# Two transformer blocks in one kernel: the order of the two kinds of weight products on TensorE

## The chip, the cores and the metric

One NeuronCore of a Trainium2 chip runs the whole program. Times are device microseconds (us) of that core. The kernel before took 2190.84 us, the median of 3 runs (2190.77 to 2191.94).

## What is computed

The input is one sequence of 256 positions with 2048 features. It passes through two residual blocks and a last RMS norm.

The first block normalises x and projects it to 3584 features. Those feed a gated causal convolution of width 3, a trailing mean minus the token followed by a small grouped product, and an attention of 4 heads over a memory of 256 positions. The memory's keys and values are a product of their own. The joined 2048 features go through `w_out` and are added to x. A feed-forward part follows: a product with 2 x 5632 columns, a causal convolution of width 3 with a bias, `silu(gate) * value`, and a product back to 2048 columns.

The second block has 8 heads of an attention over three dilated windows and 8 heads of a "difference" attention (two softmaxes, one subtracted from the other, then a norm), `w_out_2`, and a feed-forward part without the convolution.

```
x = x + mix(rmsnorm(x)) @ w_out
x = x + (silu(gate) * val) @ w_down        # gate, val = split(conv(rmsnorm(x) @ w_up))
x = x + concat(dilated(x), diff(x)) @ w_out_2
x = x + (silu(h @ w_gate) * (h @ w_up)) @ w_down
return rmsnorm(x)
```

All inputs are float32. Nearly all of the work is the weight products with 256 moving positions.

## The kernel before, in words

**Two halves for one float32 product.** Each weight block of 128 x 128 is split on the chip into an upper part (`hi`, rounded to the matmul format by a copy on ScalarE, line 175) and a lower part (`lo`, raw weight minus upper part, a subtraction on VectorE, line 187). Activations are kept as pairs too: 256 columns of upper part and 256 columns of lower part side by side, 512 columns in all. A block then needs two matmuls into one PSUM accumulator of 512 columns. The *long* one (line 208) multiplies `hi` with all 512 columns. The *short* one (line 211) multiplies `lo` with the 256 upper columns, and adds to the accumulator's second half. An accumulator's first matmul is a long one that starts it, and its last is a long one that closes it. I call a long and a short matmul on one weight block, together, a block.

**Units and quarters.** Weights come in units of 16 blocks, 1 MB each, by one DMA into `raw` (3 buffers, line 164). Half a unit, 8 blocks, is what one `hi` tile (4 buffers) and one `lo` tile (4 buffers) hold. The program is written out by hand in quarters: in each quarter, `emit_all` (lines 1009 to 1034) first lets evictions and other follow-up work that is due go out (`stage`), then the splitting of weights that are needed one or two units later, then 4 blocks of matmuls through `products`, then extra matmuls that are due (attention scores, transposes, norm sums). The queue of an engine holds its instructions in that order, and each engine works its own queue off in order.

**The order inside `products`.** It is called with the 4 blocks of a quarter. A flag, `longs`, says whether the last call ended in long matmuls or in short ones, and the next call begins with the same kind; so 4 + 4 long matmuls and 4 + 4 short ones follow one another, in runs of 8, save in quarters where an accumulator is opened or closed. There a run may be of 1, 4 or 7.

**What follows a sum.** When the quarter with the closing matmul is over, a generator (`done`, posted by `ws_units`, line 255, for the next quarter) evicts the accumulator: ScalarE copies one half, VectorE adds the other (lines 416 to 418), and further steps go out in later quarters. For residual sums VectorE alone does it (lines 742 and 743). `ready` keeps evictions back until a norm's factor is there. The accumulators are 4 PSUM buffers. The order of the products of a stage (`late_order`) takes the last two inputs of the first two sums late, so that the stage before can finish them.

**Attention of the second block.** Heads are started at fixed quarters (`t0`, lines 959 and 965), beside the next stages' products. The value products use another form (`vs_unit`, lines 275 to 277) that isn't touched.

Of the kernel before, what the change touches and what calls it, by code (L numbers as in the profile page):

```python
# [10 lines left out]
F32 = mybir.dt.float32  # L11
# [7 lines left out]
P = 128  # L19
D = 2048  # L20
S = 256
KT = D // P
# [4 lines left out]
UB = 16  # L27
EPS = 1e-6
SUBLN_EPS = 1e-5
WINDOWS = (2, 4, 8, 16)  # L30
PAD = 16
POOL_PAIRS = ((0, (0, 1)), (1, (0, 1, 2)), (2, (1, 2)), (3, (3, 4)), (4, (3, 4, 5)), (5, (4, 5)))
# [37 lines left out]
def constants():  # L70
    k = np.zeros((P, NK), np.float32)
    k[:, K_IDENT:K_IDENT + P] = np.eye(P, dtype=np.float32)
    for j in range(6):
        for p in range(P):
            w = WINDOWS[(j * P + p) // 192]
            k[p, K_INVK + j] = 1.0 / w
# [23 lines left out]
def tile_two_blocks(ctx: ExitStack, tc: tile.TileContext, a: dict, out: bass.AP):  # L100
    nc = tc.nc
    pool = lambda name, bufs, **kw: ctx.enter_context(tc.tile_pool(name=name, bufs=bufs, **kw))
    cst = pool("cst", 1)
    wraw_p = pool("wraw", 3)
    whi_p = pool("whi", 4)
    wlo_p = pool("wlo", 4)
    big = pool("big", 1)
    t1 = pool("t1", 14)
# [3 lines left out]
    sm = pool("sm", 4)  # L112
    acc_p = pool("acc", 4, space=PSUM)
# [17 lines left out]
        return vec[:, c:c + 1]  # L131

    units = []
    posts = {}
    extras = {}
    running = []

    def post(t, fn):


        posts.setdefault(t, []).append(fn)
# [48 lines left out]
    def weights(i, c0, c1):  # L190
        j = 2 * i + c0 // HB
        hi, lo = halves[j]
        c = slice(c0 % HB, (c1 - 1) % HB + 1)
        return hi[:, c], lo[:, c]

    def add_unit(src, width, emit):
        units.append((src, width, emit))
        return len(units) - 1

    longs = [True]  # L200

    def products(blocks):


        mm = nc.tensor.matmul

        def long(acc, hi, lo, x, first, last):
            mm(acc, lhsT=hi, rhs=x, start=first, stop=last)  # L208

        def short(acc, hi, lo, x, first, last):  # L210
            mm(acc[:, S:], lhsT=lo, rhs=x[:, :S], start=False, stop=False)  # L211

        opening = [b for b in blocks if b[4]]
        closing = [b for b in blocks if b[5]]
        between = [b for b in blocks if not b[4] and not b[5]]
        if longs[0] and not closing:
            for b in opening + between:
                long(*b)
            for b in blocks:
                short(*b)  # L220
            longs[0] = False
        else:
            for b in opening:
                long(*b)
            if opening and not closing:
                for b in between:
                    long(*b)
            for b in blocks:
                short(*b)
            if not opening or closing:  # L230
                for b in between:
                    long(*b)
            for b in closing:
                long(*b)
            longs[0] = bool(closing) or not opening

    def ws_units(src, blocks, done, ready=0):


        accs = {}  # L240
        for u in range(0, len(blocks), UB):
            part = blocks[u:u + UB]

            def emit(i, q, part=part):
                group = []
                for b, (m, mov, st, sp) in list(enumerate(part))[4 * q:4 * q + 4]:
                    if st:
                        accs[m] = acc_p.tile([P, 2 * S], F32, tag="acc", name="acc")
                    group.append((accs[m], *weights(i, b * P, (b + 1) * P), mov(), st, sp))
                products(group)  # L250

            i = add_unit(src[u // UB], len(part) * P, emit)
            for b, (m, _, _, sp) in enumerate(part):
                if sp:
                    post(max(4 * i + b // 4 + 1, ready), lambda m=m: done(m, accs.pop(m)))

    act_movs = [lambda kt=kt: A[:, kt, :] for kt in range(KT)]

# [22 lines left out]
    def vs_units(src, act, done, ready=0):  # L281
        accs = []
        for g in range(KT // 4):
            i = vs_unit(src[g], act, g, accs)
        for t in range(2):
            post(max(4 * i + 4, ready) + t, lambda t=t: done(t, accs[t]))

    def rsqrt_small(src, n, scale, eps):

        v = sm.tile([P, n], F32, tag=f"rs_v{n}", name="rs_v")  # L290
        y = sm.tile([P, n], F32, tag=f"rs_y{n}", name="rs_y")
        t = sm.tile([P, n], F32, tag=f"rs_t{n}", name="rs_t")
        nc.vector.tensor_scalar(out=v, in0=src, scalar1=scale, scalar2=eps, op0=ALU.mult, op1=ALU.add)
        nc.vector.tensor_scalar(out=y.bitcast(I32), in0=v.bitcast(I32), scalar1=-0.5, scalar2=float(0x5F3759DF),
                                op0=ALU.mult, op1=ALU.add)
        for _ in range(3):
            nc.vector.tensor_tensor(out=t, in0=y, in1=y, op=ALU.mult)
            nc.vector.scalar_tensor_tensor(out=t, in0=t, scalar=-0.5, in1=v, op0=ALU.mult, op1=ALU.mult)
            nc.vector.scalar_tensor_tensor(out=y, in0=t, scalar=1.5, in1=y, op0=ALU.add, op1=ALU.mult)
        return y  # L300

    class Norm:
# [3 lines left out]
        def __init__(self, name, tag="sq"):  # L306
            self.sq = big.tile([P, S], F32, tag=tag, name=f"sq_{name}", bufs=1)
            self.R = big.tile([P, S], F32, tag="R", name=f"R_{name}", bufs=2)
            self.n, self.apart = 0, False
# [24 lines left out]
        def solve(self):  # L334
            self.r = rsqrt_small(self.ps[:, 0:2], 2, 1.0 / D, EPS)
# [22 lines left out]
    class TwoNorms(Norm):  # L358
# [13 lines left out]

        def solve(self):
            r1 = self.r1 = rsqrt_small(self.ps[:, 2:4], 2, 1.0 / D, EPS)
            ms = sm.tile([P, 2], F32, tag="ms", name="ms")
            nc.vector.tensor_tensor(out=ms, in0=self.ps[:, 0:2], in1=r1, op=ALU.mult)
            nc.vector.tensor_tensor(out=ms, in0=ms, in1=r1, op=ALU.mult)
            r2 = rsqrt_small(ms, 2, 1.0 / D, EPS)
            self.r = sm.tile([P, 2], F32, tag="r12", name="r12", bufs=1)
            nc.vector.tensor_tensor(out=self.r, in0=r1, in1=r2, op=ALU.mult)  # L380
# [40 lines left out]
    def scaled(acc, R, dst=None):  # L421
        z = yield from whole(acc)
        d = z if dst is None else dst
        nc.vector.tensor_tensor(out=d, in0=z, in1=R, op=ALU.mult)  # L424
        return d
# [51 lines left out]
    M = big.tile([P, KT, 2 * S], F32R, tag="mix", name="M")  # L477
# [99 lines left out]
    def mem_v_done(t, acc):  # L577
        nc.scalar.activation(v_sb(t), acc, AF.Copy, scale=n_mem.r[:, t:t + 1])

    k_accs, v_accs = [], []  # L580
    for g in range(4):
        vs_unit(a["w_v"][g], lambda: M, g, v_accs)

        def emit(i, b, g=g):
            kt = 4 * g + b
            if kt == 0:
                for _ in range(2):
                    ac = acc_p.tile([P, 2 * S], F32, tag="acc", name="acc")
                    k_accs.append(ac)
                for _ in range(2):  # L590
                    ac = s_p.tile([P, 2 * S], F32, tag="s", name="acc_s")
                    k_accs.append(ac)
            products([(k_accs[m], *weights(i, (4 * b + m) * P, (4 * b + m + 1) * P), M[:, kt, :],
                       kt == 0, kt == KT - 1) for m in range(4)])

        i = add_unit(a["w_k"][g], UB * P, emit)
    for t in range(2):
# [64 lines left out]
    def pooled(j, acc):  # L662
        v, s, o = pads
        lo_w = WINDOWS[(j * P) // 192]
        hi_w = WINDOWS[(j * P + P - 1) // 192]
        yield from scaled(acc, n_x.R, v[:, PAD:])
# [22 lines left out]
        yield from put_pair(pooled_hl[j], pf)  # L689

    ws_units(a["w_in"][4:], full_blocks(range(6), act_movs, 0), pooled, ready=r_x)


# [195 lines left out]
    def head_b(h, t0):  # L889
# [36 lines left out]
        def s5():  # L926
# [5 lines left out]
            yield  # L932
            r = rsqrt_small(su, 2, 1.0 / P, SUBLN_EPS)
            for t in range(2):
# [21 lines left out]

    for c in range(2):
        vs_units(a["w_vb"][4 * c:], lambda: A, keep_v(1024 + 512 * c), ready=r_a)
    t0 = 4 * len(units) + 11
    for h in range(8):  # L960
        head_b(h, t0 + 11 * h)
    ws_units(a["w_qkb"], full_blocks(range(16), act_movs), rope("b"))
    for c in range(2):
        vs_units(a["w_va"][4 * c:], lambda: A, keep_v(512 * c))
    t0 = 4 * len(units) + 11
    for h in range(8):
        head_a(h, t0 + 8 * h)
    ws_units(a["w_qka"], full_blocks(range(16), act_movs), rope("a"))
# [40 lines left out]
    def emit_all():  # L1009
        nc.vector.memset(ones, 1.0)  # L1010
        first_units()
        n = len(units)
        for t in range(4 * n):
            i, q = divmod(t, 4)
            if q == 0:
                prefetch(i + 3)
            if q == 2:
                split_hi(2 * i + 4)
            stage(t)
            if q == 0 and i:  # L1020
                split_lo(2 * i + 2)
                split_hi(2 * i + 3)
            elif q == 1 and i:
                split_lo(2 * i + 3)
            units[i][2](i, q)
            for fn in extras.pop(t, ()):
                fn()
        t = 4 * n
        while posts or extras or running:
            stage(t)  # L1030
            for fn in extras.pop(t, ()):
                fn()
            t += 1
        finish()
# [96 lines left out]
```

## Time and profile before

| | |
|---|---|
| median of 3 runs | 2190.84 us (2190.77 to 2191.94) |
| the profiled execution | 2190.65 us, span 2188.8 us |
| TensorE busy | 2169.9 us, 99% of the span |
| weight loads (PEld) | 1896.8 us, 87% |
| VectorE (DVE) | 1600.6 us, 73% |
| ScalarE (ACT) | 1143.9 us, 52% |
| GpSimd (POOL) | 108.2 us, 5% |
| DMA | 408.99 MB, 187 GB/s on average |

Busy time is an engine's own; PE and PEld overlap. Matmuls are pipelined: a row's duration is longer than the time from its start to the next one's start, so spacing is read from starts. A row of the order in time joins equal instructions that follow one another ("x8"); its second column runs from the first start to the last end.

### The profile page before, as it was taken

What the parts mean: (1) busy time and instruction counts of PE and PEld (TensorE: products, weight loads), DVE (VectorE), ACT (ScalarE), POOL (GpSimd) and SP (SyncE); (2) the same over time, 40 slices, a digit from 0 to 9 for tenths busy, and PEclk for the clock granted to TensorE, in tenths of its full rate; (3) what the DMA queues carried; (4) which work ended last, traced back from release to release, by engine and by line L of the source; (5) the groups of instructions that cost most, each with busy time, mean ns of one, the idle gap of its engine ahead of it and who ended that gap; (6) DMA issues with size and microseconds to landing.
All of it is one profiled execution on the core that took longest, in us unless ns stands there. A gap on an engine that the chain in (4) does not pass through costs nothing.

```text
span 2188.8 us, 31334 instructions
## 1 busy us (share of the span) xinstructions
PE 2169.9 (99%) x12426; PEld 1896.8 (87%) x12426; DVE 1600.6 (73%) x2553; ACT 1143.9 (52%) x1738; POOL 108.2 (5%) x114
## 2 busy tenths in 40 slices
PE   8999999999999999999999999999999999999997
PEld 7888888888888888888888888888888888888886
DVE  8877778886588758888779677786665666666666
ACT  6555556664466535665456655455543445344442
POOL 4100010000000000003100000010000000000012
PEclk9999999999999999999999999999999999999998
DMA  7555555555555555555544444555555555555553
GB/s 284 201 171 180 191 188 196 191 192 191 193 192 192 193 184 193 190 185 192 193 167 160 156 172 154 175 199 189 191 190 193 193 192 193 192 192 189 189 184 113
DMA packets 60195, 408.99 MB, mean 187 GB/s; under 512 B 6672, under 2 KB 8592, under 8 KB 11792
## 3 DMA queue, kind: packets, MB, share of 16 engines
q1 hardware_dynamic: 60048, 406.99, 53.9%
q8 instruction: 97, 1.59, 0.3%
q14 instruction: 50, 0.41, 0.0%
HBM read 404.86 MB, written 2.10 MB: 186 GB/s over the span
## 4 chain that ended last, share of the span: by engine, by line
PE 97%; DVE 1%; DMA 1%; issue 0%; ACT 0%; DVEq 0%; SPq 0%; ACTq 0%
PE acc L208 60%; PE acc L211 30%; PE acc L275 1%; PE acc L276 1%; PE acc L277 1%; PE s_ps L432 1%; DMA raw<-in_w_k 1%; DVE lo L187 0%; PE pT_ps L468 0%; PE o_ps L922 0%; PE o_ps L880 0%; DVE M L545 0%; DVE end L1000 0%; DVE M L546 0%; PE nps L344 0%; DMA mem<-in_mem 0%
## 5 line engine op out<-in xcount | busy, mean ns | idle before, releaser
L175 ACT ACTIVATE hi<-raw 128x1024 fp32r<-128x1024 f32 x758 | 800.1, 1058 | 580.1 <-PE acc L208 405.5
L187 DVE TENSOR_TENSOR lo<-raw,hi 128x1024 fp32r<-128x1024 f32 x758 | 931.8, 1237 | 144.7 <-ACT hi L175 133.0
L208 PE MATMUL acc<-A,hi 128*128 128x512 f32 x3776 | 957.2, 393 | 0.0
L208 PEld LDWEIGHTS acc<-A,hi 128*128 128x128 f32 x3776 | 673.3, 188 | 115.5 <-issue 1.0
L211 PEld LDWEIGHTS acc<-A,lo 128*128 128x128 f32 x3776 | 509.3, 188 | 40.9 <-issue 0.7
L211 PE MATMUL acc<-A,lo 128*128 128x256 f32 x3776 | 523.4, 279 | 0.0
L208 PE MATMUL acc<-hid,hi 128*128 128x512 f32 x1408 | 360.1, 392 | 0.0
L208 PEld LDWEIGHTS acc<-hid,hi 128*128 128x128 f32 x1408 | 250.5, 188 | 41.4
L416 ACT ACTIVATE z<-acc 128x256 f32<-128x256 f32 x244 | 91.9, 382 | 262.4 <-PE acc L208 262.0
L211 PEld LDWEIGHTS acc<-hid,lo 128*128 128x128 f32 x1408 | 195.4, 188 | 17.3
L211 PE MATMUL acc<-hid,lo 128*128 128x256 f32 x1408 | 199.7, 279 | 0.0
L742 DVE TENSOR_TENSOR X<-acc,X 128x256 f32<-128x256 f32 x128 | 54.0, 422 | 177.4 <-PE acc L208 177.3
L418 DVE TENSOR_TENSOR z<-acc,z 128x256 f32<-128x256 f32 x244 | 103.1, 423 | 95.3 <-ACT z L416 89.6
L717 DVE SCALAR_TENSOR_TENSOR c<-z,vec,c 128x255 f32<-128x255 f32 (+1 forms) x188 | 90.0, 480 | 5.1 <-ACT c L712 1.1
L406 DVE TENSOR_TENSOR hid<-hid 128x256 fp32r<-128x256 f32 x88 | 37.4, 425 | 76.3 <-ACT hid L404 76.3
L424 DVE TENSOR_TENSOR z<-z,R_ffn 128x256 f32<-128x256 f32 x176 | 75.0, 426 | 6.0
L208 PE MATMUL acc<-y,hi 128*128 128x512 f32 x256 | 65.5, 394 | 0.0
L319 POOL TENSOR_TENSOR sq_attn<-sq_attn,sqt 128x256 f32<-128x256 f32 x30 | 29.5, 994 | 701.6 <-ACT sqt L317 701.5
L208 PE MATMUL acc<-mix,hi 128*128 128x512 f32 x256 | 64.2, 392 | 0.0
L394 ACT ACTIVATE A<-X,vec 128x256 fp32r<-128x256 f32 x64 | 32.5, 508 | 57.8 <-DVE X L743 57.3
L743 DVE TENSOR_TENSOR X<-acc,X 128x256 f32<-128x256 f32 x128 | 54.3, 425 | 4.4
L397 DVE SCALAR_TENSOR_TENSOR A<-X,vec,A 128x256 fp32r<-128x256 f32 x64 | 51.1, 810 | 8.3 <-ACT A L394 8.3
(174 smaller groups left out, 1352.6 us busy)
## 6 DMA issues: line engine op xcount, KB each, us to landing
raw<-in_w_up SPq DMA_DIRECT2D x88, 1024.0 KB, 4.8
raw<-in_w_down SPq DMA_DIRECT2D x88, 1024.0 KB, 4.9
raw<-in_w_gu SPq DMA_DIRECT2D x88, 1024.0 KB, 4.9
raw<-in_w_out SPq DMA_DIRECT2D x32, 1024.0 KB, 4.9
raw<-in_w_in SPq DMA_DIRECT2D x22, 1024.0 KB, 4.9
raw<-in_w_qkb SPq DMA_DIRECT2D x16, 1024.0 KB, 4.8
raw<-in_w_qka SPq DMA_DIRECT2D x16, 1024.0 KB, 4.9
raw<-in_w_vb SPq DMA_DIRECT2D x8, 1024.0 KB, 4.8
```

Source lines behind the costliest of these rows:

```text
L175: nc.scalar.activation(hi[:, :n], raws[i][:, c0:c0 + n], AF.Copy)
L187: nc.vector.tensor_tensor(out=lo[:, :n], in0=raws[i][:, c0:c0 + n], in1=hi[:, :n].bitcast(F32), op=ALU.subtract)
L208: mm(acc, lhsT=hi, rhs=x, start=first, stop=last)
L211: mm(acc[:, S:], lhsT=lo, rhs=x[:, :S], start=False, stop=False)
L397: nc.vector.scalar_tensor_tensor(out=a[:, kt, S:], in0=x, scalar=g, in1=hi.bitcast(F32), op0=ALU.mult, op1=ALU.subtract)
L406: nc.vector.tensor_tensor(out=hl[:, S:], in0=src, in1=h.bitcast(F32), op=ALU.subtract)
L416: nc.scalar.activation(z, acc[:, S:], AF.Copy)
L418: nc.vector.tensor_tensor(out=z, in0=acc[:, :S], in1=z, op=ALU.add)
L424: nc.vector.tensor_tensor(out=d, in0=z, in1=R, op=ALU.mult)
L717: nc.vector.scalar_tensor_tensor(out=c[:, s:], in0=z[:, :S - s], scalar=w[2 - s], in1=c[:, s:], op0=ALU.mult, op1=ALU.add)
L742: nc.vector.tensor_tensor(out=dst, in0=acc[:, :S], in1=X[:, m, :], op=ALU.add)
L743: nc.vector.tensor_tensor(out=dst, in0=acc[:, S:], in1=dst, op=ALU.add)
```

## The change

Matmuls no longer go out call by call. `products` puts each block's long and short matmul into two waiting lists and issues from them in turns: 6 long ones, then 5, 5 or 8 short ones (in rotation, 18 of each kind in a round). A turn that finds nothing to issue waits for the next call, unless the stage ends (`flush`) or only the other kind can go on. A short matmul can go when its accumulator is open; at most 3 accumulators are open; a closing long matmul waits until the shorts of its sum are out, and long ones of the next sum may pass it. An accumulator's eviction is posted when its closing matmul has been issued (`now["t"] + 1`). The tile pool of the upper parts has 5 buffers in place of 4. The subtraction for a unit's second half is written one quarter later (`q == 2`). The heads of both attentions of the second block begin 2 quarters later. A small tile, `ms`, has 1 buffer in place of 4.

```diff
+LONG_RUN = 6
+SHORT_RUNS = (5, 5, 8)
+OPEN_SUMS = 3
-    whi_p = pool("whi", 4)
+    whi_p = pool("whi", 5)
...
-    longs = [True]
-    def products(blocks):
...
+    waiting = {True: [], False: []}
+    opened = set()
+    runs = {"long": True, "left": LONG_RUN, "n": 0}
+    def turn():
+        runs["long"] = not runs["long"]
+        if runs["long"]:
+            runs["left"] = LONG_RUN
+        else:
+            runs["left"] = SHORT_RUNS[runs["n"] % len(SHORT_RUNS)]
+            runs["n"] += 1
+    def candidate(long):
+        for b in waiting[long]:
+            if not long:
+                return b if b["sum"] in opened else None
+            if b["first"]:
+                return b if b["sum"].tile is not None or len(opened) < OPEN_SUMS else None
+            if b["sum"] in opened and not (b["last"] and any(o["sum"] is b["sum"] for o in waiting[False])):
+                return b
+        return None
+    def multiply(b, long):
+        waiting[long].remove(b)
+        s = b["sum"]
+        if not long:
+            nc.tensor.matmul(s.acc()[:, S:], lhsT=b["lo"], rhs=b["x"][:, :S], start=False, stop=False)
+            return
+        opened.add(s)
+        nc.tensor.matmul(s.acc(), lhsT=b["hi"], rhs=b["x"], start=b["first"], stop=b["last"])
+        if b["last"]:
+            opened.remove(s)
+            if s.done is not None:
+                s.done()
+    def products(blocks, flush=False):
+        for b in blocks:
+            for long in (True, False):
+                waiting[long].append(b)
+        while waiting[True] or waiting[False]:
+            long = runs["long"]
+            b = candidate(long)
+            if b is None:
+                if not flush and not any(o["first"] or not long for o in waiting[long]):
+                    return
+                if candidate(not long) is None:
+                    assert not flush
+                    return
+                turn()
+                continue
+            multiply(b, long)
+            runs["left"] -= 1
+            if not runs["left"]:
+                turn()
...
+                        def issued(s=s, m=m):
+                            post(max(now["t"] + 1, ready), lambda: done(m, s.tile))
...
-            ms = sm.tile([P, 2], F32, tag="ms", name="ms")
+            ms = sm.tile([P, 2], F32, tag="ms", name="ms", bufs=1)
...
-    t0 = 4 * len(units) + 11
+    t0 = 4 * len(units) + 13
...
-            elif q == 1 and i:
+            elif q == 2 and i:
                 split_lo(2 * i + 3)
```

## Rows read from the trace of the kernel before

**Rows 1.** The page: busy times and instructions, and the last chain by line.

```profile
PE 2169.9 (99%) x12426; PEld 1896.8 (87%) x12426; DVE 1600.6 (73%) x2553; ACT 1143.9 (52%) x1738; POOL 108.2 (5%) x114
...
PE acc L208 60%; PE acc L211 30%; PE acc L275 1%; PE acc L276 1%; PE acc L277 1%; PE s_ps L432 1%; DMA raw<-in_w_k 1%; DVE lo L187 0%; PE pT_ps L468 0%; PE o_ps L922 0%; PE o_ps L880 0%; DVE M L545 0%; DVE end L1000 0%; DVE M L546 0%; PE nps L344 0%; DMA mem<-in_mem 0%
```

**Rows 2.** Stretches by stage: length, busy us (instructions) by engine, clock, DMA share, GB/s.

```profile
494.15:582.44 88.29, 88.29 (x514) 77.74 (x512) 50.54 (x67) 35.28 (x35) 0.00 (x0) 1.00 0.55 189
...
968.92:1046.48 77.56, 77.56 (x449) 68.16 (x448) 68.01 (x93) 46.32 (x76) 26.41 (x28) 1.00 0.53 185
...
1351.52:1443.45 91.93, 91.93 (x534) 80.90 (x532) 72.33 (x117) 46.78 (x72) 9.64 (x13) 1.00 0.51 177
...
1709.10:1863.55 154.45, 154.45 (x897) 135.99 (x896) 101.92 (x139) 76.52 (x110) 0.00 (x0) 1.00 0.56 192
```

**Rows 3.** The short matmuls, line 211: duration ns min/median/max, first and last start.

```profile
L211 PE MATMUL acc<-A,lo x3776: 275/279/467, 59.8 to 2094.6; 128*128 128x256 f32 x199
...
L211 PE MATMUL acc<-hid,lo x1408: 275/279/283, 495.1 to 2172.1; 128*128 128x256 f32 x176
...
L211 PE MATMUL acc<-mix,lo x256: 276/279/283, 229.4 to 315.7; 128*128 128x256 f32 x128
...
L211 PE MATMUL acc<-y,lo x256: 275/279/365, 1352.4 to 1442.4; 128*128 128x256 f32 x128
```

**Rows 4.** TensorE in order of time: start us, length us, line, operation, count.

```profile
1584.09 2.00 PE L208 MATMUL acc<-A,hi 128*128 128x512 f32 x8
1585.92 1.07 PE L211 MATMUL acc<-A,lo 128*128 128x256 f32 x8
1586.83 1.99 PE L208 MATMUL acc<-A,hi 128*128 128x512 f32 x8
1588.65 1.11 PE L211 MATMUL acc<-A,lo 128*128 128x256 f32 x8
1589.60 0.62 PE L208 MATMUL acc<-A,hi 128*128 128x512 f32 x2
```

**Rows 5.** The same view seven pairs of rounds later, with runs of 4.

```profile
1622.68 2.00 PE L208 MATMUL acc<-hid,hi 128*128 128x512 f32 x8
1624.51 0.62 PE L211 MATMUL acc<-hid,lo 128*128 128x256 f32 x4
1624.96 1.07 PE L208 MATMUL acc<-hid,hi 128*128 128x512 f32 x4
1625.88 1.10 PE L211 MATMUL acc<-hid,lo 128*128 128x256 f32 x8
1626.82 2.00 PE L208 MATMUL acc<-hid,hi 128*128 128x512 f32 x8
```

**Rows 6.** Groups by line, 1585.92 to 1586.80: count | busy us, mean ns | idle before.

```profile
L211 PE MATMUL acc<-A,lo 128*128 128x256 f32 x8 | 1.1, 276 | 0.0
```

**Rows 7.** Groups by line, 1588.66 to 1589.58.

```profile
L211 PE MATMUL acc<-A,lo 128*128 128x256 f32 x8 | 1.1, 280 | 0.0
```

**Rows 8.** TensorE in order of time, with a run of 6 short matmuls.

```profile
227.36 0.84 PE L211 MATMUL acc<-A,lo 128*128 128x256 f32 x6
228.04 0.62 PE L208 MATMUL acc<-A,hi 128*128 128x512 f32 x2
228.50 0.85 PE L208 MATMUL acc<-mix,hi 128*128 128x512 f32 x3
```

**Rows 9.** All engines in order of time, at the start of the last gate stage.

```profile
1447.39 1.21 DVE L187 TENSOR_TENSOR lo<-raw,hi 128x1024 fp32r<-128x1024 f32 x1
...
1448.50 1.10 PE L211 MATMUL acc<-A,lo 128*128 128x256 f32 x8
```

**Rows 10.** Waits of the weight loads: total us, times, longest us.

```profile
PEld acc L211 <- DVE lo L187: 3.3, 2, 2.7
```

**Rows 11.** All engines in order of time, at the end of the kernel.

```profile
2170.69 0.73 POOL L319 TENSOR_TENSOR sq_end<-sq_end,sqt 128x256 f32<-128x256 f32 x1 [4.03 <-ACT sqt L317]
...
2173.15 0.28 PE L326 MATMUL nps<-ones,sq_end 128*128 128x1 f32 x2
```

More of the change, by code (lines that the diff above doesn't have):

```diff
@@ L133, in tile_two_blocks @@
     units = []
+    now = {}
     posts = {}
@@ L198, in add_unit @@
         return len(units) - 1
-    longs = [True]
-    def products(blocks):
[L205 to L221, printed above, removed]
-        else:
[L223 to L235, printed above, removed]
+    waiting = {True: [], False: []}
@@ L237, in ws_units, with __init__, acc, block @@
+    class Sum:
+        def __init__(self, done=None, acc=None):
+            self.done = done
+            self.tile = acc
+        def acc(self):
+            if self.tile is None:
+                self.tile = acc_p.tile([P, 2 * S], F32, tag="acc", name="acc")
+            return self.tile
+    def block(s, hi, lo, x, first, last):
+        return {"sum": s, "hi": hi, "lo": lo, "x": x, "first": first, "last": last}
     def ws_units(src, blocks, done, ready=0):
-        accs = {}
+        sums = {}
@@ L241, in ws_units, with emit @@
         for u in range(0, len(blocks), UB):
             part = blocks[u:u + UB]
-            def emit(i, q, part=part):
+            def emit(i, q, part=part, u=u):
                 group = []
@@ L247, in emit @@
                     if st:
[L248 to L255, printed above, removed]
+                        sums[m] = s = Sum()
+                        def issued(s=s, m=m):
+                            post(max(now["t"] + 1, ready), lambda: done(m, s.tile))
+                        s.done = issued
+                    group.append(block(sums[m], *weights(i, b * P, (b + 1) * P), mov(), st, sp))
+                products(group, u + 4 * q + 4 >= len(blocks))
+            add_unit(src[u // UB], len(part) * P, emit)
     act_movs = [lambda kt=kt: A[:, kt, :] for kt in range(KT)]
@@ L578, in mem_v_done @@
         nc.scalar.activation(v_sb(t), acc, AF.Copy, scale=n_mem.r[:, t:t + 1])
-    k_accs, v_accs = [], []
+    k_accs, v_accs, k_sums = [], [], []
     for g in range(4):
@@ L592, in emit @@
                     k_accs.append(ac)
-            products([(k_accs[m], *weights(i, (4 * b + m) * P, (4 * b + m + 1) * P), M[:, kt, :],
-                       kt == 0, kt == KT - 1) for m in range(4)])
+                k_sums.extend(Sum(acc=ac) for ac in k_accs)
+            products([block(k_sums[m], *weights(i, (4 * b + m) * P, (4 * b + m + 1) * P), M[:, kt, :],
+                            kt == 0, kt == KT - 1) for m in range(4)], True)
         i = add_unit(a["w_k"][g], UB * P, emit)
@@ L964, in tile_two_blocks @@
         vs_units(a["w_va"][4 * c:], lambda: A, keep_v(512 * c))
-    t0 = 4 * len(units) + 11
+    t0 = 4 * len(units) + 13
     for h in range(8):
@@ L1013, in emit_all @@
         for t in range(4 * n):
+            now["t"] = t
             i, q = divmod(t, 4)
```

## The prediction

> **What bounds the kernel.** I read the page's first part, then its chain, then a table by stage, then TensorE's rows in order of time. TensorE is busy for 99% of the span, and the last chain runs through it: 60% on the long matmuls of line 208, 30% on the short ones of line 211 [rows 1]. In each stage TensorE is busy for all of it, at the full granted clock, 1.00 of 2.4 GHz [rows 2]. Nothing waits on the path, so only the spacing of matmuls, from one start to the next, can give time. The weight loads waited for a lower part twice in the whole run [rows 10].
>
> The spacing isn't one number per kind. In the regular stretch, long 8, short 8, long 8, short 8 [rows 4], the starts give 1.83 and 1.82 us for 8 long matmuls, 0.91 us for the first 8 short ones and 0.95 us for the second: 229 ns for a long one, and 114 or 119 ns for a short one. No idle time stands between, so the same instruction runs at two speeds by where it comes. The group view agrees: the first run's mean duration is 276 ns, the second's 280 [rows 6, 7]. A duration exceeds the spacing by the same modelled end (276 - 114 = 162 ns), so the median of 279 for each kind of short matmul [rows 3] says that the slow speed is at least as frequent as the fast one.
>
> What decides between them? Fast and slow alternate when both runs are 8 long. The long matmuls' single starts, which the rows join, are spaced a few ns unevenly around 229, in a pattern that seems to recur after three; 8 is not a multiple of 3, so each long run ends one place further in that cycle or starts it again. The run of 4 tests it [rows 5]: 4 short ones at 1624.51 take 0.45 us (fast, 113 ns), then 4 long ones, and the next 8 short ones take 0.94 us (slow), though fast and slow would otherwise have alternated in the same way after 8. After that slow turn come 8 long ones and again a slow turn from 1628.66, because the cycle restarts elsewhere. So the place in the cycle at which long turns to short decides, and not the run of short ones itself: quick turns were 4, 6 (0.68 us, 113 ns [rows 8]) and 8 long. This is inferred from the rows; no mechanism behind it is shown.
>
> **The change part by part.**
>
> *Turns.* Six is two periods. If a long run starts where a quick short turn leaves it, it ends where the one before ended, and the next short run is fast again. Worked through by the code, turns break only at the ends of the 21 stages, some 930 of 980 long runs have six, and the short ones are 5, 5 and 8 as written. A quick turn of 5 does not stand in the trace; 4, 6 and 8 do, and I take 5 to be like them.
>
> Price: a regular pair of rounds takes 5.51 us for 16 blocks; seven of them take 1622.68 - 1584.09 = 38.59 us, 5.513 each [rows 4, 5]. Making the slow turn fast saves 8 x 4 ns by the means [rows 6, 7], or 0.04 us by the starts: 0.036 us. So 16 blocks take 5.477 us, 342.3 ns for one. The undisturbed gate stage takes 154.45 us for 448 blocks, 344.75 each [rows 2]. The difference is 2.45 ns. There are 3776 + 1408 + 256 + 256 = 5696 such blocks [rows 3] (those of the start, which waits for its weights, left out): 14.0 us. From both sides: at most, each short matmul falls from 279 - 162 = 117 to 114 ns (by unrounded starts nearer 116 and 113), 3 x 5696 = 17 us; at least, nothing, if the place isn't held.
>
> *Places where the cycle is lost.* A stage's end, a norm, a score, a transpose or an attention output comes between. There are about 80 such breaks: 8 heads x 4, 8 x 3, 4 x 3, and 12 for the norms. One costs at most two slow turns, 13 short matmuls x 4 to 5 ns = 0.06 us, so 0 to 5 us against the 14. I take 1.5, since half of these matmuls are slow before, too.
>
> *The subtraction written a quarter later.* A quarter is 4 blocks, 4 x 344.75 ns = 1.38 us. It moves one VectorE instruction (1.21 us [rows 9]) behind the evictions of one more quarter; behind it on VectorE are the next evictions, and the next weight DMA on SP's queue, which overwrites the raw buffer it reads. Its reader comes four quarters later in place of five, and the short turns run up to two quarters behind their call, which gives the time back. In most stages VectorE is idle for much of the time (50.54 of 88.29 us busy) and it costs nothing. The tightest cover is at the stage start at 1443 us: a lower part ends at 1448.60 and the fifth matmul of the run from 1448.50, at 1448.97, reads it: 0.36 us left [rows 9]. VectorE's backlog there comes from the stage before, 72.33 us busy in 91.93 [rows 2]. Cost: 0 to 2 us; I take 1, a wait like those of rows 10 (3.3 us in two).
>
> *The fifth buffer of upper parts, evictions posted up to two quarters later, heads two quarters later, one buffer of `ms`.* The buffer lets the long turns lag; ScalarE, 52% busy [rows 1], gets its slot earlier. Four accumulators, three of them open at once: an accumulator is wanted again after three more sums, at least 3 x 8 blocks x 0.345 = 8.3 us, against evictions of about 1 us. The heads' instructions only move. At the end, the sum before the last closes some 3 us before the last in place of about 4; its square is added by GpSimd at 2171.42, 1.7 us before the matmul that reads it [rows 11], and this shrinks to about 0.5 but doesn't end. All at 0; if the cover of the last goes, 1 us.
>
> Sum: 14.0 - 1.5 - 1.0 = 11.5 us off the profiled execution's 2190.65 (span 2188.8, 1.85 around it): 2179.1; the median of the three runs is 0.2 higher. The gain's upper bound is 17, and both deductions may be zero, so I go a little lower: **2178 us**.
>
> **A rule against it.** The Trainium skill, page "TensorE: Matmul & The Clock Gate", section "Back-to-back issue gap", gives the isolated spacing at full clock as columns / 2.4 + 2.5 ns, 215.8 ns for 512 and 109.2 ns for 256, with no dependence on order. By that rule turns would change nothing, and the time would stay at 2190.7. The trace disagrees in size (229, and 114 or 119) and in kind, since one shape has two spacings [rows 4].
>
> **The rivals.**
>
> *The place isn't held (nothing moves).* Whether a short run is fast depends on something else, such as the run's length (5 not like 4 and 6) or the buffers' addresses, which the fifth buffer shifts. For it: the cycle is an inference, there is no run of 5, and of 6 short there is one. If only turns of 8 are fast, 8 of 18, the share is about what it is now. Against it: three lengths are fast with the same spacing. Time: 2190.7, or with the 1 us of waits 2191.7; if half of the gain comes, 2184. That order has no part in it at all, the two speeds following something else in time, also ends at 2190.7; with two runs of 8 at two speeds some 3 us apart in the same stage, I give this 3 in 100 of the rival's 17.
>
> *VectorE becomes the bound (slower).* Place: the two stages in which it is busy for 88% and 79%, 968.92 to 1046.48 and 1351.52 to 1443.45 [rows 2], with 14 and 16 units. If the lead of a unit's second half falls by the quarter, from 0.36 us to -1.02, TensorE waits 1 us in each of the 30 units: 2178 + 30 = 2208, since the wait also loses the place in the cycle. It decides from 13 such units on, where the gain is eaten. Against it: the narrow lead stands at one stage's start only, and the lag of the short turns adds to it.
>
> *Turns don't form,* because long matmuls find nothing to issue. Then runs stay short and irregular, and the time as for the first rival. By the code, a turn waits for its next call rather than giving way, so I give this 2 in 100, within the next figure.
>
> **How the numbers follow.** Forecast 0.76 (2173 to 2183 by its own bounds: 2190.65 - 17 to the gain less 5 and 2 us of cost), the place half or not held 0.17, VectorE's bound 0.07. A difference of over 0.2%, 4.4 us, can be told from no change here: faster means below 2186.5. The forecast is all there, and the half-held case at 2184, about 0.04: faster 0.80. Within 0.2%: 0.13. Slower: 0.07. The range from 2173 to 2187 takes in the half-held case and leaves out some 2 in 10.
>
> **What would show it.** Right: TensorE's rows show long 6 and short 5, 5, 8, with starts 0.57 and 0.91 us apart for the short turns; their mean duration is 276 in place of 279; the stages of 448 and 256 blocks take 153.4 and 87.6 us in place of 154.45 and 88.29; TensorE's waits for lower parts stay at two or three. Wrong: turns as written with means still at 279, or short turns of 5 at 119 ns and those of 8 at 113; waits of the weight loads on line 187's subtraction in many units; evictions that hold up an opening long matmul.

## The result, and the profile after

The changed kernel takes 2179.14 us, the median of 4 runs (2178.46 to 2180.35), against 2191.03 of the kernel before in the same comparison: a ratio of 0.9946, with a 95% interval from 0.9928 to 0.9963. The forecast was 2178, its sum 2179.1. The profiled execution took 2178.46 us, its span 2176.7: 12.1 us less than before.

The page's first part, of the kernel after, says the same in the busy time; the instructions are as many as in [rows 1]:

```profile
PE 2156.5 (99%) x12426; PEld 1884.5 (87%) x12426; DVE 1582.5 (73%) x2553; ACT 1119.7 (51%) x1738; POOL 125.6 (6%) x114
```

TensorE is still busy for 99% of a shorter span, so its spacing must have changed. TensorE in order of time, kernel after (start us, length us, line, operation, count; line 236 is the long matmul now, 233 the short one):

```profile
1584.55 1.07 PE L233 MATMUL acc<-A,lo 128*128 128x256 f32 x8
1585.46 1.54 PE L236 MATMUL acc<-A,hi 128*128 128x512 f32 x6
1586.83 0.73 PE L233 MATMUL acc<-A,lo 128*128 128x256 f32 x5
1587.40 1.54 PE L236 MATMUL acc<-A,hi 128*128 128x512 f32 x6
1588.77 0.73 PE L233 MATMUL acc<-A,lo 128*128 128x256 f32 x5
1589.34 1.53 PE L236 MATMUL acc<-A,hi 128*128 128x512 f32 x6
1590.71 1.07 PE L233 MATMUL acc<-A,lo 128*128 128x256 f32 x8
```

The turns are there as written. The short turn of 8 takes 1585.46 - 1584.55 = 0.91 us, each of 5 takes 0.57: 114 ns apiece in all of them, where [rows 4] had 114 and 119 by turns. Six long ones take 1.37 us, 229 ns apiece as before. What has changed is that the slower of the two short spacings has become rare. Counted from the single starts behind the first 60 us, and without the few short matmuls spaced by 130 ns or more, 57% of them were spaced by more than 115.5 ns before, and 12% are now. The short line's durations (ns min/median/max, first and last start) agree; [rows 3] had a median of 279 in each row:

```profile
L233 PE MATMUL acc<-A,lo x3776: 276/276/285, 59.2 to 2083.9; 128*128 128x256 f32 x199
...
L233 PE MATMUL acc<-hid,lo x1408: 276/276/283, 493.7 to 2160.6; 128*128 128x256 f32 x176
...
L233 PE MATMUL acc<-mix,lo x256: 276/276/280, 229.7 to 315.9; 128*128 128x256 f32 x128
...
L233 PE MATMUL acc<-y,lo x256: 276/276/285, 1346.5 to 1436.5; 128*128 128x256 f32 x128
```

Where the 12.1 us come from is read from the same four stretches of both kernels: start and first mixing part, `w_out` and first feed-forward, attention of the second block with `w_out_2`, second feed-forward. Stretches of the kernel before (length, busy us by engine as in [rows 2]):

```profile
0.00:228.50 228.50, 222.90 (x1231) 192.55 (x1232) 185.66 (x315) 130.74 (x227) 32.43 (x37) 0.99 0.60 208
228.50:1046.48 817.98, 817.98 (x4745) 720.05 (x4744) 626.30 (x924) 451.60 (x642) 37.62 (x43) 1.00 0.55 191
1046.48:1443.45 396.97, 396.97 (x2210) 340.02 (x2208) 306.76 (x643) 219.30 (x410) 12.71 (x16) 1.00 0.50 170
1443.45:2173.15 729.70, 729.70 (x4233) 642.35 (x4232) 472.98 (x654) 341.46 (x460) 21.44 (x16) 1.00 0.54 186
```

The same view of the kernel after, and below it single stages: one of 256 blocks, the one with the busiest VectorE, the one of 448 blocks, and the two with attention heads beside them:

```profile
0.00:228.57 228.57, 221.74 (x1231) 192.06 (x1231) 184.49 (x316) 129.06 (x227) 30.14 (x37) 0.99 0.60 208
228.57:1040.50 811.93, 811.93 (x4745) 714.54 (x4744) 617.68 (x923) 438.08 (x641) 47.91 (x42) 1.00 0.57 192
1040.50:1436.88 396.38, 396.38 (x2209) 338.81 (x2208) 306.69 (x643) 215.83 (x410) 19.04 (x16) 1.00 0.50 170
1436.88:2160.97 724.09, 724.09 (x4234) 637.18 (x4232) 464.72 (x654) 335.97 (x459) 24.46 (x17) 1.00 0.55 188
...
492.59:580.22 87.63, 87.63 (x513) 77.09 (x512) 50.91 (x67) 34.98 (x36) 0.00 (x0) 1.00 0.56 190
963.79:1040.50 76.71, 76.71 (x449) 67.50 (x448) 68.74 (x94) 45.56 (x76) 28.03 (x27) 1.00 0.58 192
...
1700.79:1854.16 153.37, 153.37 (x897) 134.98 (x896) 99.71 (x139) 74.45 (x109) 0.00 (x0) 1.00 0.57 194
...
1087.08:1188.24 101.16, 101.16 (x609) 86.83 (x608) 84.97 (x213) 59.99 (x132) 0.00 (x0) 1.00 0.46 157
1241.46:1344.51 103.05, 103.05 (x599) 90.64 (x598) 77.99 (x159) 54.84 (x104) 0.00 (x0) 1.00 0.50 171
```

The second and fourth stretch, where nearly nothing comes between the products, give 6.05 + 5.61 = 11.66 us on 4480 blocks, 2.60 ns a block. The first and third, with the other 1216 counted blocks, give -0.07 and 0.59. The gain stands where the turns run undisturbed, and nearly nowhere else: of the short matmuls there 56% were slow before and 4% are now, and in the first and third stretch (behind the first 60 us) it is 60% before and 42% now, by the same count.

### The profile page after: what moved, and what is told of

Its sections match the earlier page's. It is cut to its first block, busy times and chain, and to the rows that moved or that the text cites. A ratio compares the mean times of both kernels' runs of the same rounds, so it can differ in the third digit from the quotient of the medians.

```text
span 2176.7 us, 31598 instructions
## 1 busy us (share of the span) xinstructions
PE 2156.5 (99%) x12426; PEld 1884.5 (87%) x12426; DVE 1582.5 (73%) x2553; ACT 1119.7 (51%) x1738; POOL 125.6 (6%) x114
## 4 chain that ended last, share of the span: by engine, by line
PE 96%; DVE 2%; DMA 1%; ACT 0%; issue 0%; SPq 0%; DVEq 0%; ACTq 0%
PE acc L236 60%; PE acc L233 30%; PE acc L317 1%; PE acc L318 1%; PE acc L319 1%; PE s_ps L474 1%; DVE lo L192 1%; DMA raw<-in_w_v 1%; DVE A L439 0%; PE pT_ps L510 0%; PE o_ps L965 0%; PE o_ps L923 0%; DMA raw<-in_w_k 0%; DVE end L1043 0%; ACT hi L180 0%
## 5 line engine op out<-in xcount | busy, mean ns | idle before, releaser
L192 DVE TENSOR_TENSOR lo<-raw,hi 128x1024 fp32r<-128x1024 f32 x758 | 931.5, 1240 | 112.0 <-PE acc L233 64.8
L236 PE MATMUL acc<-A,hi 128*128 128x512 f32 x3776 | 986.1, 393 | 0.0
L180 ACT ACTIVATE hi<-raw 128x1024 fp32r<-128x1024 f32 x758 | 789.5, 1053 | 375.5 <-PE acc L236 272.7
L236 PEld LDWEIGHTS acc<-A,hi 128*128 128x128 f32 x3776 | 662.6, 188 | 101.4 <-issue 1.7
L233 PEld LDWEIGHTS acc<-A,lo 128*128 128x128 f32 x3776 | 524.1, 188 | 53.9
L233 PE MATMUL acc<-A,lo 128*128 128x256 f32 x3776 | 534.0, 277 | 0.0
L785 DVE TENSOR_TENSOR X<-acc,X 128x256 f32<-128x256 f32 x128 | 54.1, 422 | 164.8 <-PE acc L236 164.4
L446 ACT ACTIVATE hid<-hid 128x256 fp32r<-128x256 f32 x88 | 36.7, 417 | 130.4 <-DVE hid L850 130.4
L361 POOL TENSOR_TENSOR sq_ffn<-sq_ffn,sqt 128x256 f32<-128x256 f32 x30 | 39.3, 1310 | 615.4 <-ACT sqt L359 615.3
L757 ACT ACTIVATE c<-z,vec 128x256 f32<-128x256 f32 x88 | 53.0, 602 | 22.2 <-DVE z L466 21.2
L361 POOL TENSOR_TENSOR sq_end<-sq_end,sqt 128x256 f32<-128x256 f32 x14 | 20.3, 1451 | 697.7 <-ACT sqt L359 697.7
```

The lines of the kernel that those rows point to most:

```text
L180: nc.scalar.activation(hi[:, :n], raws[i][:, c0:c0 + n], AF.Copy)
L192: nc.vector.tensor_tensor(out=lo[:, :n], in0=raws[i][:, c0:c0 + n], in1=hi[:, :n].bitcast(F32), op=ALU.subtract)
L233: nc.tensor.matmul(s.acc()[:, S:], lhsT=b["lo"], rhs=b["x"][:, :S], start=False, stop=False)
L236: nc.tensor.matmul(s.acc(), lhsT=b["hi"], rhs=b["x"], start=b["first"], stop=b["last"])
L361: nc.gpsimd.tensor_tensor(out=self.sq, in0=self.sq, in1=q, op=ALU.add)
L446: nc.scalar.activation(h, src, AF.Copy)
```

## The experiments

The theory after the result: a long turn ends at one of three places of a cycle; from one of them the short matmuls behind it are spaced by 113 to 114 ns (a quick turn), from the other two by 118 (a slow turn); long turns of six keep the good place. The rivals: the waiting lists, the fifth buffer or the later postings give the time; or 5, 5, 8 matter in themselves. In the short diffs below the base is the changed kernel, save for one. Each ratio is against the kernel before on the same chip.

**Turns of 8 and 8.**

```diff
-LONG_RUN = 6
-SHORT_RUNS = (5, 5, 8)
+LONG_RUN = 8
+SHORT_RUNS = (8,)
```

> The changed kernel with turns of 8 long and 8 short matmuls. Theory (the place in a cycle of three at which a long run ends decides the speed of the short run behind it): 8 is not a multiple of three, so every second short run is slow again, as before the change: about 2190 us (2187 to 2193), the undisturbed 448-block stage at 154.4 us, the mean spacing of a short matmul near 116 ns. Rival (the waiting lists, the fifth buffer or the later postings give the time, not the length of the turns): stays at 2179 us and 153.4 us.

Measured: 2189.20 us, ratio 0.9994 (0.9985 to 1.0002). TensorE in order of time, and the 448-block stage in the table by stage, of this kernel:

```profile
1585.13 1.11 PE L233 MATMUL acc<-A,lo 128*128 128x256 f32 x8
1586.08 2.00 PE L236 MATMUL acc<-A,hi 128*128 128x512 f32 x8
1587.91 1.07 PE L233 MATMUL acc<-A,lo 128*128 128x256 f32 x8
1588.82 0.39 PE L236 MATMUL acc<-A,hi 128*128 128x512 f32 x1
```

```profile
1707.60:1861.97 154.37, 154.37 (x897) 135.94 (x896) 100.80 (x139) 72.70 (x109) 0.00 (x0) 1.00 0.56 193
```

Short turns of 0.95 and 0.91 us alternate again, as in [rows 4], and the stage is back at 154.4 us. Lists, buffer and postings are all still in; without the turn of six they give nothing that this can tell. This is what the theory says.

**All but the turns.** This one starts from the kernel before.

```diff
-    whi_p = pool("whi", 4)
+    whi_p = pool("whi", 5)
...
-    t0 = 4 * len(units) + 11
+    t0 = 4 * len(units) + 13
...
-            elif q == 1 and i:
+            elif q == 2 and i:
```

(and one buffer of `ms`)

> The kernel before, in its own order of matmuls, with all the rest of the change: fifth buffer of upper parts, the second subtraction a quarter later, heads two quarters later, one buffer of ms. Theory: nothing on the path, 2191 us (2189 to 2193), 448-block stage at 154.4 us. Rival (the fifth buffer shifts addresses or frees a wait, and gives part of the time): 2186 us or less.

Measured: 2191.24 us, ratio 1.0001 (0.9992 to 1.0010). The same stage of this kernel takes 154.45 us, to the hundredth what it took in [rows 2]:

```profile
1709.92:1864.37 154.45, 154.45 (x897) 136.00 (x896) 100.84 (x139) 72.52 (x109) 0.00 (x0) 1.00 0.56 193
```

The fifth buffer and the moved instructions cost nothing and give nothing by themselves, as far as the interval can tell. The later postings hang on the waiting lists and are not in this run; they are in the one before.

**Turns of 6 and 6.**

```diff
-SHORT_RUNS = (5, 5, 8)
+SHORT_RUNS = (6,)
```

> The changed kernel with turns of 6 long and 6 short ones, no 5 or 8. Theory: only the long run's length counts, a quick short run of any length hands the place on, so 2179 us (2177 to 2182), 448-block stage at 153.4 us, short ones near 113.5 ns. Rival (5, 5, 8 are needed, the short runs' lengths set the place too): clearly over 2183 us, with short matmuls near 116 ns or more.

Measured: 2196.64 us, ratio 1.0024 (1.0015 to 1.0034): slower than before the change, and the expectation missed by 17.6 us. Three stages of this kernel in the table by stage, of 256, 448 and 224 blocks:

```profile
1626.44:1714.08 87.64, 87.64 (x514) 77.10 (x512) 50.04 (x65) 34.94 (x35) 0.00 (x0) 1.00 0.56 193
1714.08:1870.36 156.28, 156.28 (x898) 136.97 (x896) 99.22 (x139) 74.63 (x109) 0.00 (x0) 1.00 0.55 190
1870.36:1947.03 76.67, 76.67 (x450) 67.47 (x448) 45.13 (x61) 31.14 (x31) 0.00 (x0) 1.00 0.55 191
```

Two of the three are as good as with 5, 5, 8 (87.63 and 76.71), and the one between is worse than before the change (154.45 [rows 2]). TensorE in order of time, in the first stage and in the second:

```profile
1640.59 1.54 PE L236 MATMUL acc<-hid,hi 128*128 128x512 f32 x6
1641.97 0.84 PE L233 MATMUL acc<-hid,lo 128*128 128x256 f32 x6
1642.65 1.54 PE L236 MATMUL acc<-hid,hi 128*128 128x512 f32 x6
...
1740.35 0.87 PE L233 MATMUL acc<-A,lo 128*128 128x256 f32 x6
1741.06 1.55 PE L236 MATMUL acc<-A,hi 128*128 128x512 f32 x6
1742.44 0.87 PE L233 MATMUL acc<-A,lo 128*128 128x256 f32 x6
```

In the first, each short turn takes 1642.65 - 1641.97 = 0.68 us, 113 ns apiece; in the second 0.71, 118 apiece, and it stays so for the whole stage (99% of its short matmuls, by the count above). The long matmuls of that stage are slower, too, 230.8 ns on average against 228.9 in the first. Six and six have more than one steady state. The single spacings, worked out from the starts in the trace, show them (ns; long | short; the last long one's is up to the first short one's start):

```
good place held  (1579.30 us, changed kernel):   226 229 232 225 230 231 | 114 113 113 114 113
wrong place held (1589.92 us, turns of 6 and 6): 234 235 230 231 226 229 | 120 118 117 119 117 118
wrong place held ( 865.00 us, turns of 6 and 6): 229 232 226 229 231 226 | 118 118 118 117 118 118
```

The cycle of three, about 226, 229, 232, is in all of them. Where the long turn ends on 231 or 232, the short one is quick; where it ends on 229 or 226, it is slow. The traces of all ten kernels bear this out (short turns of three or more directly behind a long one, after the first 60 us): of 5173 behind an ending from 230.5 to 233 ns 98% are quick, and of 3075 behind a smaller one 99% are slow; 242 behind a longer one, nearly all slow, are left out. So the length of the long turn decides where a turn that begins well ends, as forecast. What the theory lacked is how a stage that begins badly gets out: a slow short turn moves the place by its own length, and a slow one of 6 leaves it where it was. The two wrong places don't cost the same. In the second row the long turn itself begins slower, with 234 and 235, as it does in the stage of 156.28 us; the stage of the third row, without that, takes 155.3 us for its 448 blocks.

**Turns of 7 and 7.** `LONG_RUN = 7`, `SHORT_RUNS = (7,)`.

> The changed kernel with turns of 7 and 7. Theory: a long run of 7 that starts where a quick short run leaves it ends one place further, the short run is slow, the next long run starts with a spacing of about 235 ns and 7 later ends at the same wrong place: nearly every short run is slow. 229.8 + 118 = 347.8 ns for a block against 342.3, over some 5000 undisturbed blocks +27 us: about 2206 us (2198 to 2210), slower than before the change; 448-block stage near 155.8 us. Rival (the lists or buffers give the time): 2179 us. Rival (runs of any length but 6 fall back to half quick, half slow): 2190 us.

Measured: 2193.91 us, ratio 1.0011 (1.0002 to 1.0020): slower than before, but by a fifth of what was expected. The order in time, and the 448-block stage:

```profile
1587.11 1.76 PE L236 MATMUL acc<-A,hi 128*128 128x512 f32 x7
1588.70 0.99 PE L233 MATMUL acc<-A,lo 128*128 128x256 f32 x7
1589.53 1.78 PE L236 MATMUL acc<-A,hi 128*128 128x512 f32 x7
1591.14 0.96 PE L233 MATMUL acc<-A,lo 128*128 128x256 f32 x7
1591.94 0.39 PE L236 MATMUL acc<-A,hi 128*128 128x512 f32 x1
```

```profile
1712.35:1867.01 154.66, 154.66 (x897) 135.90 (x896) 99.62 (x139) 74.38 (x109) 0.00 (x0) 1.00 0.56 191
```

Slow turns (0.83 us) and quick ones (0.80) alternate. I had the slow turn hand on the place as a slow turn of 8 does in the kernel before (next long spacings 235, 231, 232); of 7 it hands on another (233, 236, 229), from where seven long ones end well. Turns of 8 alternate in the same way and take 154.37 us; the difference is in those longer spacings at the start of the long turn, 229.7 ns for a long one on average against 228.9 with turns of 8. This is the same gap in the theory as with 6 and 6. It says now: a quick short turn of any length hands the place on; a slow one shifts it by its length; a length that is a multiple of three can get stuck. Over the ten kernels, in which short turns come in lengths from 3 to 15, this rule names the place at which the next long turn ends in 95% of 2906 cases behind a slow turn, and in 98% of 4872 behind a quick one.

**Short turns of 4, 7, 7, and of 3, 9.** With long turns of 6 each; both lists come to six on average.

```diff
-SHORT_RUNS = (5, 5, 8)
+SHORT_RUNS = (4, 7, 7)
```

> The changed kernel with long turns of 6 and short turns of 4, 7, 7. Theory as it stands after the turns of 6 and 6 (a quick short run of any length hands the place on; a slow one shifts it by its length, and only lengths that are a multiple of three leave it where it is): the wrong place is left after a few turns in every stage, 2179 us (2177 to 2182), all 448-block stages at 153.4 us. Rival (5 and 8, which leave 2 when divided by three, are special): 2185 us or more, with stages over 155 us.

```diff
-SHORT_RUNS = (5, 5, 8)
+SHORT_RUNS = (3, 9)
```

> The changed kernel with long turns of 6 and short turns of 3 and 9. Theory: both are multiples of three, so a stage that starts at the wrong place stays there, as with 6 and 6: 2188 to 2200 us, single stages either wholly quick (448 blocks in 153.4 us) or wholly slow (155 us or more). Rival (any change of length from turn to turn frees it): 2179 us.

Measured: 4, 7, 7 takes 2179.12 us, ratio 0.9945 (0.9932 to 0.9957); 3, 9 takes 2196.06 us, ratio 1.0023 (1.0014 to 1.0032). The 448-block stage with 4, 7, 7, then the 256-block and the 448-block stage with 3, 9:

```profile
1701.09:1854.44 153.35, 153.35 (x898) 134.94 (x896) 99.83 (x139) 74.22 (x109) 0.00 (x0) 1.00 0.57 194
```

```profile
1625.30:1712.93 87.63, 87.63 (x513) 77.11 (x512) 49.92 (x65) 34.84 (x35) 0.00 (x0) 1.00 0.56 191
1712.93:1869.22 156.29, 156.29 (x898) 136.96 (x897) 100.14 (x139) 74.58 (x109) 0.00 (x0) 1.00 0.56 190
```

Both came as expected. 5 and 8 are not special; of the lists tried with long turns of six, those without a multiple of three get out of the wrong place, and the two of multiples of three alone are stuck in the same stage, at the same 156.3 us.

**Long turns of 9, short ones of 8, 8, 11.** `LONG_RUN = 9`, `SHORT_RUNS = (8, 8, 11)`. The closing matmuls come up to a quarter later than steps at fixed quarters allow for, so some of those read tiles ahead of their write. This kernel therefore doesn't compute the two blocks, and only its times are of use; instructions and shapes are the same.

> The changed kernel with long turns of 9 and short turns of 8, 8, 11. Theory: 9 is a multiple of three and 8 and 11 are not, so it does as well as 6 with 5, 5, 8: 2179 us (2176 to 2183), short matmuls near 113.5 ns in the undisturbed stages. Rival (it is something about runs of 6): 2186 us or more.

Measured: 2180.28 us, ratio 0.9950 (0.9938 to 0.9963). The 448-block stage of this kernel:

```profile
1702.34:1855.69 153.35, 153.35 (x897) 134.94 (x896) 100.82 (x139) 74.79 (x109) 0.00 (x0) 1.00 0.57 193
```

Nine does as well as six in this stage, so it is not something about runs of 6; other multiples of three were not tried. Six is the one with the smaller lag.

**A new long turn after each break.** In the stages with attention heads half of the short turns are slow in the changed kernel too, and the idea is that a score or transpose cuts a long turn at any place.

```diff
+AFTER_BREAK = {"s2": 6, "s6": 6}
...
+    def restart(n):
+        if runs["long"]:
+            runs["owed"] += n - runs["left"]
+        else:
+            runs["short"] = runs["left"]
+            runs["owed"] = n
+        runs["long"], runs["left"] = True, n
...
+            if t in extras:
+                restart(AFTER_BREAK.get(extras[t][-1].__name__, 4))
```

> The changed kernel, in which each break (score, transpose, attention output, norm) starts a new long turn: of 6 behind the transposes, of 4 behind the others; the next short turn makes up the difference. Theory: in the disturbed stages about half of the short runs are slow since a break ends the long run at a wrong place; ending it at the right one brings back up to 2 us of some 2.5: 2177.5 us (2176 to 2179), the two rope stages shorter by 0.5 us each. Rival (the breaks themselves, not the place behind them, cost it): no change, 2179 us, and the share of slow short matmuls in these stages as before.

Measured: 2178.16 us (2177.62 to 2179.29), ratio 0.9940 (0.9927 to 0.9954). Beside it on the same chip, 4, 7, 7 took 2179.12 (2178.72 to 2179.88); the runs overlap, so a gain over the changed kernel isn't shown by the times. The two stages with attention heads beside them (the rope stages of the expectation), of this kernel:

```profile
1088.27:1189.17 100.90, 100.90 (x609) 87.01 (x608) 83.45 (x209) 59.71 (x131) 0.00 (x0) 1.00 0.46 157
1242.38:1345.20 102.82, 102.82 (x599) 90.33 (x598) 76.39 (x155) 55.04 (x105) 0.00 (x0) 1.00 0.48 164
```

They are 0.26 and 0.23 us shorter than after the change (101.16 and 103.05), half of what was expected. Of their short matmuls that wait for nothing, those spaced by more than 115.5 ns fall from 55% to 38% and from 50% to 27%, counted from the single starts. So the place behind a break is part of the loss there, and my two lengths set it right only some of the time.

## Why the prediction was right, point by point

- *The bound* (spacing on TensorE, two speeds of one instruction): right. The span fell by 12.1 us, although TensorE's listed waits rose from 9.0 to 10.5 us.
- *The price of the turns*: 14.0 us for 5696 blocks at 2.45 ns. The 4480 undisturbed ones gave 2.60 ns each, 11.66 us where the term makes 11.0. The stages of 448 and 256 blocks were forecast at 153.4 and 87.6 us, and take 153.37 and 87.63. The term takes the 448-block stage for all, and the stages of 224 blocks gave more: the one from 968.92 to 1046.48 took 77.56 us [rows 2], 346.3 ns a block and not 344.75, as 70% of its short matmuls were slow; it takes 76.71 now and gave 3.8 ns a block.
- *Places where the cycle is lost*: undersized at 1.5 us. The other 1216 blocks were worth 3.0 us by the same term and gave 0.5, so 2.5 went, of which the one new wait (next point) is 0.6 at most. The reason is in the counts above: some 4 in 10 of the short matmuls in these two stretches are still slow, and about half in the two stages beside the attention heads.
- *The subtraction a quarter later*: taken at 1 us, at the start of the last gate stage. No wait came there. By the rows below (TensorE's own waits, three of the kernel before and then two of the kernel after) the one wait added behind the start is at a norm, 0.6 us. The waits for lower parts are all in the first 59 us: 4.5 us in two now (and 0.7 in three short ones), 2.3 and 2.0 before, and for the weight loads 4.9 us in two against 3.3 in two [rows 10]; that part takes as long as before. It moved one wait that I did not name: VectorE's subtraction now waits for short matmuls to release its buffer, 64.8 us in 57 times. VectorE has that time.

```profile
PE acc L211 <- DVE lo L187: 2.3, 1, 2.3
PE nps L344 <- DVE rs_y L299: 2.2, 1, 2.2
PE acc L276 <- DVE lo L187: 2.0, 1, 2.0
...
PE acc L233 <- DVE lo L192: 4.5, 2, 2.4
PE nps L386 <- DVE rs_y L341: 2.8, 2, 2.2
...
DVE lo L192 <- PE acc L233: 64.8, 57, 2.4
```

- *The fifth buffer, later postings, heads, `ms`*: at nothing, and nothing shows for them without turns of six (2191.24 us, and 2189.20 with the postings in). That the fifth buffer is what lets the turns lag is read from the code; no run has the turns without it.
- *"The place at which long turns to short decides, and not the run of short ones itself"*: half right. It holds while the place is good, and that was enough for the time. But that 5 is "like 4 and 6" is not so for slow turns: with 6 alone the kernel was slower than before, 2196.64 us. The forecast took 5, 5, 8 as they stood and did not see why they are not 6; its rival "the place isn't held" had the right doubt with the wrong length, for it is 6 that fails, and 5 and 8 that get out. That the list to be judged was one that gets out was luck, as far as the forecast's reasons go; by them 6 and 6 would have come out at the same time. So is part of how near the sum came: the places where the cycle is lost took 1.9 to 2.5 us in place of 1.5 and the wait 0.6 at most in place of 1, each wrong, but together the 2.5 us of the sum.
- *That order has no part, or that turns don't form*: neither. Turns of 8 and 8 leave everything else in and lose the gain. In the kernel after 893 of 1037 runs of long matmuls have six, where the forecast had some 930 of 980; a turn that a break cuts in two counts as two runs here.
- *VectorE as the bound*: did not come. In the stage where it is busiest, 68.74 of 76.71 us, TensorE is as quick as elsewhere: 342.5 ns a block.

## What to carry to other kernels

Where one engine is busy throughout, compare the spacing of the same instruction from start to start in different places: two spacings for one shape may be time that order alone can give back, as here. When a pattern locks to a good state, ask what it does from each bad one, for a list that only holds a state (6 and 6) can hold the wrong one as well. Breaks by other work disturb the state, so count the gain over undisturbed stretches only.

## What the runs showed of the hardware

- In these kernels a matmul of 512 columns behind another one, each with its own weight load, has no single spacing at the full granted clock (1.00 in the stages above) but a cycle of three, about 226, 229 and 232 ns. Matmuls of 256 columns behind such a run are spaced by 113.3 ns on average if the run ended on the third, and by 118 ns if not, for the whole run (98% and 99% of the turns counted above).
- While the good place is held, changing between the two shapes shows no cost of its own: with runs of 6 and 5 to 8 a block takes 342.3 ns (153.37 us for 448), which is 228.9 for the long matmul, the mean of the cycle, and 113.4 for the short one. Behind a slow run the next long matmuls can start with 233 to 236 ns.
- What makes the cycle stays open: no run varied anything that could tell.
